# Up projections of a two-block transformer on one Trainium2 core: weights split over PSUM, quarter sums made and stored by GpSimd, modulation weights loaded by SP

## The chip, the cores and the metric

The kernel runs on one core of one Trainium2 chip. The metric is the device time of one execution in microseconds (us). A core has TensorE (matmuls, written to PSUM), VectorE (DVE in the rows), ScalarE (ACT), GpSimd (POOL), and SyncE (SP, which here only issues DMAs). Each engine works through its own instructions in order. PEld is the loading of weights into TensorE.

## The reference

Two transformer blocks on x of 1 x 1024 x 1024, float32. Each block ends with a feed-forward part whose first matmul, the up projection, is what the change is about:

```python
# first block
h = rms_norm(x, ffn_pre_norm[l])
f = jnp.square(jax.nn.relu(h @ w_up[l])) @ w_down[l]        # w_up 1024 x 4096
x = x + rms_norm(f, ffn_post_norm[l])
# second block, with a modulation from c
mod = c @ w_ada[l] + b_ada[l]                               # w_ada 1024 x 6144, six rows of 1024
sh1, sc1, gt1, sh2, sc2, gt2 = jnp.split(mod, N_MOD, axis=-1)
h = modulate(rms_norm_2(x, g_pre_mix[l]), sh1, sc1)
...
h2 = modulate(rms_norm_2(x, g_pre_mlp[l]), sh2, sc2)
ff = jnp.square(jax.nn.relu(h2 @ w_mlp_in[l])) @ w_mlp_out[l]
x = x + gt2[:, None, :] * rms_norm_2(ff, g_post_mlp[l])
```

## The kernel before

**Products in three matmuls.** Every float32 operand is split into a high part (hi, rounded to the matmul's format) and a low part (lo, the rest). One product of two operands is hi x hi + hi x lo + lo x hi, so 3 matmuls per 128 rows of the contraction (mm3, L173). Without a scale, `split` is a ScalarE copy for hi (L178) and a VectorE subtraction for lo (L179).

**Seven products in place of eight.** Both matmuls of the feed-forward part use a 2 x 2 block scheme with seven block products and sums of blocks (Strassen's, in Winograd's form). `ffn_up` walks over 16 slabs of 256 columns of w_up (`slab`, L1061). For each slab it loads 1 MB of weights with SP (L1065), alternately into the buffers `w_raw` and `fraw`; VectorE makes four sums of weight blocks (`fws`, L1073); `halves_of` splits them and the raw blocks into the `w_hi` and `w_lo` tiles, two of each, which is one slab's worth. Then follow the products q6, q2, q7, q5, q4, q3 with 12 matmuls of 128x512 each, into the six PSUM banks of the `mm` ring. VectorE adds them up:

- u2 = x + q6 (L1098, tile `fu2`), f11 = x + q2 (L1103, tile `f00`), u3 = u2 + q7 (L1109, `fu3`), f22 = u3 + q5 (L1113, tile `f11`), f12 = u3 - q4 (L1119, in place in `fu3`), f21 = u2 + q5 + q3 (L1122, L1125, in place in `fu2`).

ScalarE applies relu and the square to f11, f22, f12, f21 (L1050, L1051). f11 and f22 are stored by ScalarE's queue. Then VectorE makes five quarter sums of the squares (L1130, tile `fs`), and SP stores each (L1043) to the scratch tensors fs0, fs4, fs6, fs1, fs5. The down projection (`ffn_down`) reads them back as left operands; there GpSimd makes the sums of weight blocks (L1173).

The products that need only b11 and b21 (p1 and q2) of the first 12 slabs (`LEAD`) are computed ahead, stored to `fx_dr` and loaded back as `fx` and `f00`. So the first 12 slabs run five products in the slab and the last four run seven.

**Buffers.** `TAGS["fp"]` gives the number of buffers of each tile in this stage: `fws`, `fraw`, `fu2`, `fu3`, `f11` have one each, `fx`, `f00`, `fs` two, `ada_acc` two, `ada_raw` one. The PSUM ring `tr` (two banks) holds transposes in other stages and is not used inside a slab.

**Modulation.** mod = c @ w_ada is made by VectorE: `modulation_acc` loads 512 KB of w_ada at a time by GpSimd's DMA queue (L1234, tile `ada_raw`) and adds up the rows weighted by c in `ada_acc` (L1238, L1240). A third runs beside the first up projection (4 column blocks, `side1`), the rest beside the qkv projections of the second block (8 blocks, `block2_conv_qkv`); both are generators that are stepped once per slab or part.

**The order.** A scheduler orders each engine's instructions when the program is built, within the dependences. An instruction that waits holds back all that stands behind it on its engine, DMA issues too.

Of the kernel before, what the change touches and what calls it, by code (L numbers as in the profile page):

```python
# [65 lines left out]
def tile_two_blocks(ctx: ExitStack, tc: tile.TileContext, I, out):  # L66
# [972 lines left out]
    def ffn_up(hq, w_up, fl, fp, first, side):  # L1039
# [20 lines left out]
        def slab(c, lead):  # L1060
# [15 lines left out]

            def halves_of(t, slots, v):
                split(t[0][:, slots], t[1][:, slots], v)

# [3 lines left out]
            if not lead:  # L1083
                halves_of(u[0], slice(2, 4), r4[:, :, 0])
            halves_of(u[0], slice(0, 2), ws[:, 0:2])
            halves_of(u[1], slice(0, 2), ws[:, 2:4])
            halves_of(u[1], 2, a22)
            if lead:
                x, f11 = (fp.tile([P, 512], F32, name=nm) for nm in ("fx", "f00"))
                for i, t in enumerate((x, f11)):  # L1090
                    SP.dma_start(t, fx_dr[:, 512 * (2 * c + i):512 * (2 * c + i) + 512])
                q2 = f11
            else:
                x = p1(fp, op(u[0], 2))
# [32 lines left out]
            for i, x, z, o in ((4, f11, f12, ALU.add), (0, f11, f22, ALU.add), (6, f12, f22, ALU.subtract),  # L1127
                               (1, f21, f22, ALU.add), (5, f21, f11, ALU.subtract)):
                t = fp.tile([P, 512], F32, name="fs")
                DVE.tensor_tensor(out=t, in0=x, in1=z, op=o)  # L1130
                left(c, i, t)

# [95 lines left out]

    def modulation_acc(i, pool, first, prev):

        acc = pool.tile([P, 512], F32, name="ada_acc")
        for q in range(4):
            raw = pool.tile([P, 2, 512], F32, name="ada_raw")
            POOL.dma_start(raw, I["w_ada_2"][0][256 * q:256 * q + 256, 512 * i:512 * i + 512]  # L1234
                           .rearrange("(k p) n -> p k n", p=P))
            for k in range(2):
                if q + k == 0:
                    DVE.tensor_scalar(acc, raw[:, 0, :], col(R_C), None, ALU.mult)  # L1238
                else:
                    DVE.scalar_tensor_tensor(out=acc, in0=raw[:, k, :], scalar=col(R_C + 2 * q + k), in1=acc,  # L1240
                                             op0=ALU.mult, op1=ALU.add)
            if q == 1:
                if i > first:
                    modulation_sum(i - 1, prev, pool)
                yield
        return acc

    def modulation_sum(i, acc, pool):
        row = pool.tile([P, 512], F32, name="f_r")[0:1, :]
        p = mm_tile()  # L1250
        PE.matmul(p[0:1, :], ones[:, 0:1], acc, start=True, stop=True)
        ACT.copy(row, p[0:1, :])
        SP.dma_start(mod_raw[i // 2:i // 2 + 1, (i % 2) * 512:(i % 2) * 512 + 512], row)
# [19 lines left out]
    def modulation(pool, m0, m1):  # L1273

        acc = None
        for i in range(2 * m0, 2 * m1):
            acc = yield from modulation_acc(i, pool, 2 * m0, acc)
            yield
        modulation_sum(2 * m1 - 1, acc, pool)
        modulation_columns(pool, m0, m1)  # L1280
        yield
# [7 lines left out]
    def block2_conv_qkv(h, w_in, pb, first, side):  # L1289
# [6 lines left out]
        def slab(c0, fn):  # L1296
            w = w_cols(w_in, c0, 256)
            for sl in halves:
                part(w, sl, fn)
                next(side, None)  # L1300

# [9 lines left out]
        for pr in range(2):  # L1311
# [5 lines left out]
            for n, sl in enumerate(halves):  # L1317
# [4 lines left out]
                if pr == 0:  # L1322
                    values(n)
                next(side, None)
            for j in range(2):
# [220 lines left out]
    with ExitStack():  # L1546
        with banks(mm=6, tr=2):
# [7 lines left out]
            def side1(fp):  # L1555
                g = modulation(fp, 0, 2)
                return lambda c: next(g, None)

# [9 lines left out]
            with sbuf("dp", 1, tags=TAGS["dp"]) as dp:  # L1568
                with sbuf("yf", 1, side="right") as yp, sbuf("ep", 1, side="right", tags="gpost xt*2 junk yg hmod*2") as ep:
# [6 lines left out]
                        lambda i: w_cols(w_in2, (1024, 512)[i], 256))  # L1576
            with sbuf("pb", 2) as pb, sbuf("pm", 1, tags="ada_acc*2 ada_raw*3 f_r") as pm:
                side = modulation(pm, 2, 6)
# [61 lines left out]
```

## Time and profile before

| | |
|---|---|
| median of 3 runs | 2814.18 us (2810.9 to 2832.78) |
| profiled execution | 2828.66 us, span of its trace 2827.0 us, granted clock 0.975 |
| TensorE busy | 2654.5 us, 94% |
| VectorE busy | 1971.4 us, 70% |
| ScalarE busy | 1309.2 us, 46% |
| GpSimd busy | 564.5 us, 20% |
| first up projection's slabs | about 720 to 1020 us |
| second up projection's slabs | about 2215 to 2500 us |

A busy TensorE is not TensorE at its peak: its matmuls are pipelined and their ends are modelled. Durations of single instructions overlap a little with the next one's. Idle time of an engine is put down to what ended it, the releaser; idle time of an engine that is not the bottleneck costs nothing.

### The profile page before, as it was taken

What the parts mean: (1) busy time and instruction counts of PE and PEld (TensorE: products, weight loads), DVE (VectorE), ACT (ScalarE), POOL (GpSimd) and SP (SyncE); (2) the same over time, 40 slices, a digit from 0 to 9 for tenths busy, and PEclk for the clock granted to TensorE, in tenths of its full rate; (3) what the DMA queues carried; (4) which work ended last, traced back from release to release, by engine and by line L of the source; (5) the groups of instructions that cost most, each with busy time, mean ns of one, the idle gap of its engine ahead of it and who ended that gap; (6) DMA issues with size and microseconds to landing.
All of it is one profiled execution on the core that took longest, in us unless ns stands there. A gap on an engine that the chain in (4) does not pass through costs nothing.

```text
span 2827.0 us, 39450 instructions
## 1 busy us (share of the span) xinstructions
PE 2654.5 (94%) x13801; PEld 2240.7 (79%) x13801; DVE 1971.4 (70%) x3614; ACT 1309.2 (46%) x2360; POOL 564.5 (20%) x568
## 2 busy tenths in 40 slices
PE   8999999999878899999999999998999889999996
PEld 7788889998756687777888788887798767778785
DVE  7668689858777775568764448777567778755666
ACT  5544666546433444345521246564257544443342
POOL 1242353200000022434210013111200000023413
PEclk9999999999989999999999999998999999999998
DMA  4296476356676467777564645443756556487785
GB/s 130 85 295 195 153 214 176 113 168 223 217 229 203 164 243 251 267 257 269 186 219 135 216 135 168 126 117 121 252 180 215 184 192 208 171 301 248 262 281 185
DMA packets 381500, 562.23 MB, mean 199 GB/s; under 512 B 39427, under 2 KB 215658, under 8 KB 381302
## 3 DMA queue, kind: packets, MB, share of 16 engines
q1 hardware_dynamic: 358262, 505.17, 54.3%
q0 software_dynamic: 6912, 25.17, 3.0%
q10 hardware_dynamic: 16128, 29.37, 2.8%
q8 instruction: 109, 1.79, 0.3%
q14 instruction: 89, 0.73, 0.1%
HBM read 408.83 MB, written 150.78 MB: 198 GB/s over the span
## 4 chain that ended last, share of the span: by engine, by line
PE 25%; DMA 17%; DVE 10%; ACT 4%; POOL 4%; issue 3%; SPq 1%; POOLq 0%; DVEq 0%; ACTq 0%
PE mm L173 21%; DMA w_raw<-in_w_down 3%; DVE w_lo L179 3%; DMA w_raw<-in_w_mlp_out 3%; POOL w_raw L1173 3%; DMA fs<-fs 2%; ACT w_hi L178 2%; DMA dwr<-in_w_mlp_out 1%; DMA dwr<-in_w_down 1%; PE po L906 1%; DVE w_lo L209 1%; POOL dwr L1173 1%; PE tr L898 1%; DMA mrg<-m_sg 1%; DMA m_sg<-sig 1%
## 5 line engine op out<-in xcount | busy, mean ns | idle before, releaser
L173 PE MATMUL mm<-w_hi,df 128*128 128x512 f32 x1792 | 559.9, 393 | 9.8 <-ACT y L1200 6.1
L173 PE MATMUL mm<-hq_t,w_hi 128*128 128x512 f32 x1280 | 411.0, 406 | 68.4 <-DVE fu L1098 61.9
L173 PEld LDWEIGHTS mm<-w_hi,df 128*128 128x128 f32 x1792 | 338.6, 189 | 83.9 <-ACT y L1200 7.3
L173 PE MATMUL mm<-w_lo,df 128*128 128x512 f32 x896 | 352.8, 394 | 8.4 <-DVE w_lo L179 8.3
L173 PEld LDWEIGHTS mm<-hq_t,w_hi 128*128 128x128 f32 x1280 | 249.4, 196 | 131.8 <-DVE fu L1098 37.7
L173 PE MATMUL mm<-h_hi,w_hi 128*128 128x512 f32 x736 | 290.9, 395 | 0.0
L173 PE MATMUL mm<-h_lo,w_hi 128*128 128x512 f32 x736 | 289.4, 393 | 0.0
L173 PE MATMUL mm<-h_hi,w_lo 128*128 128x512 f32 x736 | 289.0, 393 | 0.0
L173 PE MATMUL mm<-hq_t,w_lo 128*128 128x512 f32 x640 | 253.5, 402 | 1.6 <-DVE w_lo L179 1.6
L209 DVE TENSOR_TENSOR w_lo<-w_raw,w_hi 128x1024 fp32r<-128x1024 f32 (+1 forms) x138 | 172.5, 1273 | 98.2 <-ACT w_hi L203 97.9
L1173 POOL TENSOR_TENSOR w_raw<-w_raw 128x1024 f32<-128x1024 f32 x40 | 109.0, 2725 | 580.1 <-DMA fs<-fs 392.2
L203 ACT CAST w_hi<-w_raw 128x1024 fp32r<-128x1024 f32 (+1 forms) x138 | 139.1, 1049 | 172.3 <-PE mm L173 68.9
L173 PEld LDWEIGHTS mm<-w_lo,df 128*128 128x128 f32 x896 | 169.7, 189 | 49.0 <-DVE w_lo L179 14.2
L173 PE MATMUL mm<-w_hi,mixT 128*128 128x256 f32 x1024 | 184.9, 282 | 5.2 <-DVE m_sg L1443 2.2
L179 DVE TENSOR_TENSOR df<-dfr,df 128x1024 fp32r<-128x1024 f32 x112 | 147.1, 1324 | 56.5 <-ACT df L178 56.3
L179 DVE TENSOR_TENSOR w_lo<-dwr,w_hi 128x1024 fp32r<-128x1024 f32 x56 | 105.2, 1879 | 114.1 <-ACT w_hi L178 113.7
L1173 POOL TENSOR_TENSOR dwr<-dwr 128x1024 f32<-128x1024 f32 x40 | 99.6, 2491 | 372.4 <-DMA dwr<-in_w_mlp_out 200.5
L173 PEld LDWEIGHTS mm<-h_hi,w_hi 128*128 128x128 f32 x736 | 138.4, 188 | 33.9 <-issue 2.8
L173 PEld LDWEIGHTS mm<-w_hi,mixT 128*128 128x128 f32 x1024 | 157.7, 189 | 7.2 <-ACT w_hi L203 4.7
L173 PEld LDWEIGHTS mm<-h_hi,w_lo 128*128 128x128 f32 x736 | 138.4, 188 | 27.3
L173 PEld LDWEIGHTS mm<-h_lo,w_hi 128*128 128x128 f32 x736 | 138.4, 188 | 26.3 <-issue 0.2
L173 PE MATMUL mm<-hq,w_hi 128*128 128x512 f32 x512 | 159.2, 391 | 0.0
(415 smaller groups left out, 5850.3 us busy)
## 6 DMA issues: line engine op xcount, KB each, us to landing
dfr<-fs SPq DMA_DIRECT2D x112, 512.0 KB
fs<-fs SPq DMA_DIRECT2D x160, 256.0 KB
w_raw<-in_w_in SPq DMA_DIRECT2D x32, 1024.0 KB
ada_raw<-in_w_ada POOLq DMA_DIRECT2D x48, 512.0 KB, 5.1
w_raw<-in_w_down SPq DMA_DIRECT2D x48, 512.0 KB
dwr<-in_w_down SPq DMA_DIRECT2D x48, 512.0 KB
w_raw<-in_w_mlp_out SPq DMA_DIRECT2D x48, 512.0 KB
dwr<-in_w_mlp_out SPq DMA_DIRECT2D x48, 512.0 KB
```

Source lines behind the costliest of these rows:

```text
L173: PE.matmul(ps, l, r, start=first and n == 0, stop=final and n == last)
L178: ACT.copy(hi, src)
L179: DVE.tensor_tensor(out=lo, in0=src, in1=r32(hi), op=ALU.subtract)
L203: ins = ACT.copy(wh[:, step * i:step * i + step], raw[:, step * i:step * i + step])
L209: DVE.tensor_tensor(out=wl[:, c], in0=raw[:, c], in1=r32(wh[:, c]), op=ALU.subtract)
L898: PE.transpose(pt[:, 256 * j + P * i:256 * j + P * i + P], prob[i][:, ks], ident)
L906: PE.matmul(po[:, d:], vb if j else va, t[:, 256 * j:256 * j + 256 - d], start=n == 0 and m == 0, stop=n == len(groups) - 1 and m == 3)
L1173: POOL.tensor_tensor(out=a, in0=a, in1=b, op=ALU.subtract if sub else ALU.add)
```

## The change

Four things change, all in or beside the up projections.

- `halves_of` now works on one block of 128 x 512 at a time. ScalarE copies the block to `w_hi` and then copies `w_hi` again into a bank of the `tr` ring in PSUM; VectorE subtracts with one operand in PSUM. The order of the blocks changes: s4 is split last.
- The five quarter sums are made by GpSimd (its `tensor_tensor`) and stored from GpSimd's DMA queue. The `fs` buffers stay two.
- The modulation weights are loaded by SP. In the first up stage `ada_raw` has two buffers and `ada_acc` one.
- The modulation steps once per 512 KB load in place of once per two; the callers in `block2_conv_qkv` step it twice, and the last slab of the first up projection runs it to its end. The row of a finished block goes through an `fs` buffer in place of one of its own.

```diff
@@ TAGS
-    "fp": "fws fraw fx*2 f00*2 fu2 fu3 f11 fs*2 ada_acc*2 ada_raw f_r",
+    "fp": "fws fraw fx*2 f00*2 fu2 fu3 f11 fs*2 ada_acc ada_raw*2",
@@ slab
-            def halves_of(t, slots, v):
-                split(t[0][:, slots], t[1][:, slots], v)
+            def halves_of(t, n, v):
+
+                ACT.copy(t[0][:, n], v)
+                pt = tr_tile().rearrange("p (k n) -> p k n", k=4)
+                ACT.copy(pt, r32(t[0][:, n]))
+                DVE.tensor_tensor(out=t[1][:, n], in0=v, in1=pt, op=ALU.subtract)
...
             if not lead:
-                halves_of(u[0], slice(2, 4), r4[:, :, 0])
-            halves_of(u[0], slice(0, 2), ws[:, 0:2])
-            halves_of(u[1], slice(0, 2), ws[:, 2:4])
+                halves_of(u[0], 2, a11)
+                halves_of(u[0], 3, a12)
+            halves_of(u[0], 0, s2)
+            halves_of(u[0], 1, s3)
+            halves_of(u[1], 0, s1)
             halves_of(u[1], 2, a22)
+            halves_of(u[1], 1, s4)
...
                 t = fp.tile([P, 512], F32, name="fs")
-                DVE.tensor_tensor(out=t, in0=x, in1=z, op=o)
-                left(c, i, t)
+                POOL.tensor_tensor(out=t, in0=x, in1=z, op=o)
+                left(c, i, t, POOL)
@@ modulation_acc
             raw = pool.tile([P, 2, 512], F32, name="ada_raw")
-            POOL.dma_start(raw, I["w_ada_2"][0][256 * q:256 * q + 256, 512 * i:512 * i + 512]
+            SP.dma_start(raw, I["w_ada_2"][0][256 * q:256 * q + 256, 512 * i:512 * i + 512]
...
-            if q == 1:
-                if i > first:
-                    modulation_sum(i - 1, prev, pool)
-                yield
+            yield
@@ modulation_sum
-        row = pool.tile([P, 512], F32, name="f_r")[0:1, :]
+        row = pool.tile([P, 512], F32, name="fs")[0:1, :]
@@ block2_conv_qkv, twice
-                next(side, None)
+                next(side, None), next(side, None)
```

The scheduler moves instructions as a consequence. Three places show it. Numbers behind a name tell the tiles of one slab from those of another; lines of the changed kernel are up to 12 higher than those of before, and u2 is L1105 there.

VectorE before, first up projection, end of one slab and start of the next: the fs rows are the five quarter sums of a slab, and the L1098 row is u2 of the next.

```order
L1130 TENSOR_TENSOR fs_10522<-f00_10431,f11_10481 128x512 [waits DMAHW3_49,Activation_49]
L1130 TENSOR_TENSOR fs_10519<-f00_10431,fu3_10466 128x512 [waits DMAHW0_49,Activation_49]
L1130 TENSOR_TENSOR fs_10528<-fu2_10447,f11_10481 128x512 [waits DMAHW7_49,DVE_49,Activation_49]
L1130 TENSOR_TENSOR fs_10525<-fu3_10466,f11_10481 128x512 [waits DMAHW0_49,DVE_49]
L179 TENSOR_TENSOR w_lo_10685<-fws_10679,w_hi_10684 128x1024 [waits PE_49,Activation_49]
L1130 TENSOR_TENSOR fs_10531<-fu2_10447,f00_10431 128x512 [waits DMAHW3_49,DVE_49]
L1098 TENSOR_TENSOR fu2_10582<-fx_10565,mm_10569 128x512 [waits DVE_49]
L1109 TENSOR_TENSOR fu3_10601<-fu2_10582,mm_10588 128x512 [waits DVE_49]
```

The sums wait for the DMAs of their buffers in VectorE's own row, and u2 stands behind the last of them.

VectorE in the changed kernel, the same place in another slab, from u2 to the subtraction of f12 (L1126):

```order
L1105 TENSOR_TENSOR fu2_10089<-fx_10072,mm_10076 128x512 [waits Pool_49]
L1082 TENSOR_TENSOR w_lo_10190<-fws_10182,tr_10208 128x512 [waits Activation_49]
L1116 TENSOR_TENSOR fu3_10108<-fu2_10089,mm_10095 128x512 [waits DVE_49]
L1073 TENSOR_TENSOR fws_10327<-fraw_10325 128x512 [waits DMAHW3_49,DVE_49]
L1110 TENSOR_TENSOR f00_10212<-fx_10211,f00_10212 128x512 [waits DMAHW5_49,DMAHW1_49,DMAHW0_49]
L1073 TENSOR_TENSOR fws_10327<-fraw_10325 128x512
L1120 TENSOR_TENSOR f11_10123<-fu3_10108,mm_10110 128x512 [waits DMAHW6_49,DVE_49]
L1129 TENSOR_TENSOR fu2_10089<-fu2_10089,mm_10110 128x512
L1073 TENSOR_TENSOR fws_10327<-fws_10327,fraw_10325 128x512 [waits DVE_49]
L1126 TENSOR_TENSOR fu3_10108<-fu3_10108,mm_10128 128x512 [waits DVE_49]
```

u2 now waits for GpSimd, and here nine operations stand from u2 to f12; in the slab ahead of it five do. Over the 16 slabs the count is 7.5 on average in the first stage and 6.25 in the second.

GpSimd in the changed kernel, one slab of the first up projection and the first sum of the next (before, its row held only the loads of `ada_raw` here):

```order
L1137 TENSOR_TENSOR fs_10025<-f00_9934,f11_9984 128x512 [waits DMASW1_49,Activation_49]
L1043 DMA fs0_99<-fs_10025 128x512 [waits Pool_49]
L1137 TENSOR_TENSOR fs_10022<-f00_9934,fu3_9969 128x512 [waits DMASW7_49,Activation_49]
L1043 DMA fs4_103<-fs_10022 128x512 [waits Pool_49]
L1137 TENSOR_TENSOR fs_10031<-fu2_9950,f11_9984 128x512 [waits DMASW2_49,Activation_49]
L1043 DMA fs1_100<-fs_10031 128x512 [waits Pool_49]
L1137 TENSOR_TENSOR fs_10028<-fu3_9969,f11_9984 128x512 [waits DMASW3_49]
L1043 DMA fs6_105<-fs_10028 128x512 [waits Pool_49]
L1137 TENSOR_TENSOR fs_10034<-fu2_9950,f00_9934 128x512 [waits DMASW5_49]
L1043 DMA fs5_104<-fs_10034 128x512 [waits Pool_49]
L1137 TENSOR_TENSOR fs_10164<-f00_10073,f11_10123 128x512 [waits DMASW6_49,Activation_49]
```

Each sum waits for the store (DMASW) of an earlier one, since the five share two buffers in turn: fs4, fs6 and fs5 of this slab have the one, fs0 and fs1 the other. fs5 is the last reader of `fu2`.

## Rows read from the trace of the kernel before

**Rows 1.** The windows view, by stage; after the stretch: length, then each engine.

```profile
core 0: us, PE busy (x) PEld busy (x) DVE busy (x) ACT busy (x) POOL busy (x), PEclk, DMA share, GB/s
720.00:1020.00 300.00, 254.05 (x1039) 202.11 (x1038) 230.38 (x334) 120.33 (x185) 14.18 (x17) 0.92 0.59 195
...
1350.00:1650.00 300.00, 295.22 (x1471) 244.18 (x1469) 156.35 (x248) 80.94 (x135) 35.33 (x48) 1.00 0.57 189
2215.00:2500.00 285.00, 261.25 (x1103) 211.99 (x1102) 218.12 (x306) 125.56 (x186) 9.96 (x5) 0.97 0.57 198
```

**Rows 2.** Groups of instructions, 720 to 1020 us: busy, mean ns, idle before.

```profile
line engine op names shapes xcount | busy us, mean ns | idle before us <-releasers
L173 PE MATMUL mm<-hq_t,w_hi 128*128 128x512 f32 x608 | 196.9, 409 | 46.0 <-DVE fu L1098 41.4 <-ACT hq_t L356 3.3 <-ACT fx L1057 0.7
...
L179 DVE TENSOR_TENSOR w_lo<-fws,w_hi 128x1024 fp32r<-128x1024 f32 x32 | 39.0, 1219 | 1.3 <-ACT w_hi L178 1.3
...
L1130 DVE TENSOR_TENSOR fs<-fu,f 128x512 f32<-128x512 f32 x44 | 31.6, 730 | 30.9 <-DMA fs<-fs 30.9
...
L1098 DVE TENSOR_TENSOR fu<-fx,mm 128x512 f32<-128x512 f32 x15 | 10.3, 684 | 1.8 <-PE mm L173 1.5
...
L1057 ACT COPY fx<-mm 128x512 f32<-128x512 f32 x4 | 2.3, 583 | 2.9 <-PE mm L173 2.9
```

**Rows 3.** The chain of waits, 1460 to 1600 us: start, us, what.

```profile
1466.92 32.87 PE mm L173 x144
```

**Rows 4.** Timeline, VectorE: first and last of 16 L1098, per stage.

```profile
734.96 0.69 DVE L1098 TENSOR_TENSOR fu<-fx,mm 128x512 f32<-128x512 f32 x1 [1.50 <-PE mm L173]
...
1025.37 0.69 DVE L1098 TENSOR_TENSOR fu<-fx,mm 128x512 f32<-128x512 f32 x1
...
2216.99 0.68 DVE L1098 TENSOR_TENSOR fu<-fx,mm 128x512 f32<-128x512 f32 x1
...
2480.20 0.69 DVE L1098 TENSOR_TENSOR fu<-fx,mm 128x512 f32<-128x512 f32 x1
```

**Rows 5.** Timeline, VectorE, 874 to 882 us: start, us, line, out<-in, idle before.

```profile
874.42 0.68 DVE L1130 TENSOR_TENSOR fs<-f,f 128x512 f32<-128x512 f32 x1
...
877.22 1.42 DVE L1130 TENSOR_TENSOR fs<-fu,f 128x512 f32<-128x512 f32 x2 [1.41 <-DMA fs<-fs]
...
880.78 0.69 DVE L1130 TENSOR_TENSOR fs<-fu,f 128x512 f32<-128x512 f32 x1 [1.01 <-DMA fs<-fs]
881.51 0.69 DVE L1098 TENSOR_TENSOR fu<-fx,mm 128x512 f32<-128x512 f32 x1
```

**Rows 6.** Timeline, ScalarE, same slab.

```profile
886.28 0.62 ACT L1051 ACTIVATE fu<-fu 128x512 f32<-128x512 f32 x1
```

**Rows 7.** What tile fs waits for: us, times.

```profile
  DMA fs<-fs: 71.6, 43
```

**Rows 8.** Line 1234: duration ns min/median/max; landing of its loads; who waited.

```profile
L1234 POOL DMA_DIRECT2D ada_raw<-in_w_ada x48: 722/722/928, 730.8 to 1605.4; - x48
...
  DVE ada_acc L1240: 20.9, 15
...
DMA to landing us min/median/max: 4.0/5.1/7.7
```

**Rows 9.** Timeline from the start: SP's first 512 KB load and its reader.

```profile
0.81 0.39 SPq L254 DMA_DIRECT2D xt<-in_x  x1
...
4.41 1.06 ACT L274 ACTIVATE xj<-xt 128x1024 f32<-128x1024 f32 x1 [2.32 <-DMA xt<-in_x]
```

**Rows 10.** Line 629, GpSimd sums of 128x512: duration ns min/median/max.

```profile
L629 POOL TENSOR_TENSOR cacc<-cacc,cprod x16: 1270/1290/2377, 247.4 to 361.0; 128x512 f32<-128x512 f32 x16
```

**Rows 11.** Tile dwr: duration ns min/median/max of GpSimd sums and VectorE subtractions.

```profile
L179 DVE TENSOR_TENSOR w_lo<-dwr,w_hi x56: 1211/1226/3468, 1027.9 to 2792.8; 128x1024 fp32r<-128x1024 f32 x56
...
L1173 POOL TENSOR_TENSOR dwr<-dwr x40: 2370/2396/3288, 1022.4 to 2788.7; 128x1024 f32<-128x1024 f32 x40
```

**Rows 12.** The page, groups: the same subtraction's mean over the run.

```profile
L179 DVE TENSOR_TENSOR w_lo<-dwr,w_hi 128x1024 fp32r<-128x1024 f32 x56 | 105.2, 1879 | 114.1 <-ACT w_hi L178 113.7
```

More of the change, by code (lines that the diff above doesn't have):

```diff
@@ L1226, in ffn_down, with modulation_acc @@
         return res
-    def modulation_acc(i, pool, first, prev):
+    def modulation_acc(i, pool):
         acc = pool.tile([P, 512], F32, name="ada_acc")
@@ L1276, in modulation @@
         for i in range(2 * m0, 2 * m1):
-            acc = yield from modulation_acc(i, pool, 2 * m0, acc)
-            yield
+            if acc is not None:
+                modulation_sum(i - 1, acc, pool)
+            acc = yield from modulation_acc(i, pool)
         modulation_sum(2 * m1 - 1, acc, pool)
@@ L1323, in block2_conv_qkv @@
                     values(n)
-                next(side, None)
+                next(side, None), next(side, None)
             for j in range(2):
@@ L1556, in side1, with step @@
                 g = modulation(fp, 0, 2)
-                return lambda c: next(g, None)
+                def step(c):
+                    next(g, None)
+                    if c == 15:
+                        for _ in g:
+                            pass
+                return step
             mx1 = ExitStack()
@@ L1576, in tile_two_blocks @@
                         lambda i: w_cols(w_in2, (1024, 512)[i], 256))
-            with sbuf("pb", 2) as pb, sbuf("pm", 1, tags="ada_acc*2 ada_raw*3 f_r") as pm:
+            with sbuf("pb", 2) as pb, sbuf("pm", 1, tags="ada_acc*2 ada_raw*3 fs") as pm:
                 side = modulation(pm, 2, 6)
```

## The prediction, made before the changed kernel was run

> **What bounds the kernel now.** I read the windows view first, for the two stretches that the change touches: the up projection of the first block (720 to 1020 us) and of the second (2215 to 2500 us) [rows 1]. TensorE is busy 254 of 300 us and 261 of 285 us there, and its granted clock is 0.92 and 0.97 of full speed, a mean over its two levels (1.2 and 2.4 GHz). Elsewhere at full clock one 128x512 matmul takes 32.87/144 = 0.228 us [rows 3], so the 1039 and 1103 matmuls of these windows need 237 and 252 us. 63 and 33 us are lost, 96 us together: that is all that any relief of the other engines can win here.
>
> Then the groups of the first window, for what TensorE waits for. 41.4 of the 46.0 us of idle time before the hq_t matmuls end with VectorE's L1098 [rows 2], the first sum of a slab (u2 below). u2 starts 16 times in a stage, from 734.96 to 1025.37 us and from 2216.99 to 2480.20 us [rows 4]: 15 steps of 19.4 us and 15 of 17.5 us. One slab of the first twelve has five products of 12 matmuls, 60 x 0.228 = 13.7 us; one of the last four has seven, 19.2 us. So the early slabs are paced by something else than TensorE.
>
> It is not VectorE's throughput alone: 230 of 300 us are busy [rows 1], about 14 us of a 19.4 us step. Part of the rest is the wait for a free fs buffer, 71.6 us in 43 waits over both stages [rows 7], 30.9 of them before one group in the first window [rows 2]. The timeline of one slab shows how that runs [rows 5]: a sum at 874.42, the next use of its buffer at 877.22, once its store has landed, another wait before 880.78, and only then, behind it in VectorE's row, u2 of the next slab at 881.51.
>
> **The change part by part.**
>
> Quarter sums. Five leave VectorE per slab: 5 x 0.69 us [rows 2], and the waits before them. On GpSimd a 128x512 sum takes 1.29 us [rows 10] and a DMA issue 0.72 us [rows 8], so 5 x 2.01 = 10 us of engine time per slab: it fits a step of 17 us. But fu2 has one buffer and its last reader is the fifth sum, so in the changed order u2 waits for GpSimd, and the sums alternate on two fs buffers. That makes a ring, which I cost as follows:
> - From u2 to the squared f12: 881.51 [rows 5] to 886.28 + 0.62 = 886.90 [rows 6], 5.4 us, where five VectorE operations lie from u2 to the subtraction of f12.
> - Then fs4 needs f12, fs6 needs fs4's buffer back, fs5 needs fs6's buffer back, and u2 needs fs5: three sums, 3.9 us, and two returns of a buffer, 2K. K is the time from a sum's end to its store landed.
> - So a step is 9.3 us + 2K. Operations that the new order puts between u2 and f12 add 0.6 us each. It has 7.5 places on average in the first stage and 6.25 in the second, instead of five: 1.5 and 0.75 us. Half the slabs have a copy and a cast of ScalarE among the squares too, 2 x 0.58 us [rows 2]: 0.5 us on average.
>
> K for a store of 256 KB by GpSimd stands in no row. From below: SP's store took from 874.42 + 0.68 to 877.22, 2.1 us [rows 5]. From above: GpSimd's loads of 512 KB land 5.1 us after issue in the median [rows 8]. Between them: GpSimd's quickest 512 KB load took 4.0 us [rows 8], SP's first one 4.41 - 0.81 = 3.6 us [rows 9], so GpSimd's way costs some 0.4 us more: 2.5 us unhindered. Under this load the median is 5.1/4.0 of the quickest: 3.2 us, and 0.1 us for the hand-over. I take K = 3.3 us, nearer the store than the load, since bytes and direction are the store's.
> The Trainium skill (DMA: Bandwidth & Descriptors, section Anatomy of one DMA) gives a GpSimd DMA 2.0 us + bytes/436e3, an estimate of 2.6 us for 256 KB and 3.2 us for 512 KB; this trace does not agree, its quickest 512 KB load is 4.0 us. By the page's 2.6 us the sum below would be 42 us lower.
>
> With K = 3.3 the steps are 9.3 + 6.6 + 1.5 + 0.5 = 17.9 us and 17.15 us. Against 19.4 and 17.5 us over 15 steps each: -22 us and -6 us.
>
> Subtractions from PSUM. VectorE took 1.22 us for 1024 columns [rows 2]; now it takes two of 512 at the 0.68 us of an operation with one PSUM operand (L1098) [rows 2]. With five slots in an early slab that is 3.4 us for 3.1 us: no relief. ScalarE adds five copies; the nearest row is 0.58 us (PSUM read, 128x512) [rows 2], so 2.9 us, and some 0.4 us for the split casts. No row has ScalarE writing to PSUM; bounds 0 and twice that, 1.16 us each, and I take the row. ScalarE is busy 120 of 300 us [rows 1], 8 us of a step, so it is then at 11 to 14 us and still off the path: cost 0. VectorE falls to about 11 us a slab, plus 1.5 us of modulation in the first stage.
>
> Modulation weights. 48 issues leave GpSimd for SP. Two raw buffers in the first stage could save the waits of VectorE, 20.9 us in both modulations [rows 8]; if the ring paces, they are not on the path: 0, and at best -13 us. SP gains 16 loads in the first stage and loses 80 stores in each, which waited there for VectorE. A load of ada_raw at SP's head that waits for VectorE holds w_up behind it; the ring's slack (17 against 13.7 us) covers one such wait of 3 us. In the second modulation (1350 to 1650 us) TensorE is busy 295 of 300 us and VectorE 156 [rows 1]: nothing is late, 0; without that cover the 32 loads would cost 0.4 us of SP each.
>
> The end of the up stage. Ten sums of the last two slabs now stand in GpSimd's row among the first eight weight sums of the down projection (2.4 us each [rows 11]). A weight sum can be kept by one store's return and one sum, 3.3 + 1.3 us; I count 5 us per stage, ends 0 and 10: +10 us.
>
> Sum: -22 - 6 + 10 = -18 us. On the profiled execution's own 2828.66 us (span 2827.0 us) that is 2811 us. The median of the runs is 2814.18 us, 14.5 us lower, so there it is **2796 us**, -0.6%. About 1%, 28 us, is what a measurement of this kernel can tell from no change.
>
> **The rivals.**
>
> *The stores return quickly.* K near 2.5 us: thirty steps lose 2 x 0.8 us each, 48 us more, 2748 us. For it: stores no longer share SP's queue with loads of 1 MB, and SP's own took 2.1 us. Against it: the loaded median of GpSimd's loads. Its end is TensorE's pace, all 96 us: 2718 us. Here the step would be VectorE's 11 us or TensorE's 13.7 us, and GpSimd would only have moved work off.
>
> *The stores return slowly: slower than before.* One mechanism, K: each us is 60 us of the kernel. It turns the sign at K = 3.6 us and passes 1% slower at K = 4.1 us. With 4.5 us, still below the median of the 512 KB loads, the time is 2868 us. For it: GpSimd issues only after its own sum, so that the issue's 0.72 us lies inside K, where SP's overlapped VectorE's next work. Against: half the bytes.
>
> *Sums and VectorE hold each other.* VectorE's w_lo over dwr takes 1226 ns in the median and 3468 ns at most [rows 11], 1879 ns on average [rows 12], while GpSimd's sums run beside it and stretch from 2396 to 3288 ns [rows 11]: 0.65 us per operation. In an early slab the operations with two SBUF operands are four fws sums and one f00 sum; some two of five lie between u2 and f12, 2 x 0.65 us x 30 = 39 us, 2835 us. Against it: the subtractions and the other sums read PSUM.
> The Trainium skill (SBUF — State Buffer, section Who interferes with whom) says that a VectorE instruction with two SBUF inputs contends with a GpSimd instruction that reads SBUF; the stretched rows agree.
>
> *The change does not do what it says*: if VectorE were the bound, the PSUM subtractions would not relieve it (3.4 for 3.1 us); only the sums do.
>
> **How the numbers follow.** Ring at K between 3.1 and 4.1 us, 2786 to 2842 us, likeliest 2796: chance 0.38. Quick stores: 0.35. Slow stores: 0.17. Contention on top of the forecast: 0.10, of which 0.06 stay within 1%. So faster 0.35, within 1% 0.44, slower 0.21. The range leaves out a tenth on either side: K below 2.45 us, 2745 us, and K above 4.2 us, 2850 us.
>
> **What would show it.** After the change: u2 preceded by idle time that ends with GpSimd's fs; GpSimd's sums preceded by idle time that ends with their own stores; u2's steps near 17.9 and 17.2 us; VectorE some 100 us less busy (160 sums at 0.69 us); TensorE still idle behind u2. Steps of 14 to 15 us would prove the ring quick. The forecast is wrong if u2 does not wait for GpSimd, if K is outside 3.1 to 4.1 us, or if ScalarE's copies come last before the matmuls.

## The result, and the profile after

The changed kernel took 2897.01 us in the median of 4 runs (2887.93 to 2906.47), the kernel before 2817.55 us in 4 runs beside it (2810.9 to 2832.78): a ratio of 1.0275, 95% interval 1.0218 to 1.0332. It is slower by 2.8%, above the upper end of the range (2850 us), where 2796 us had been forecast. The profiled execution has a span of 2890.4 us, against 2827.0 us before: 63.4 us more. Medians and ratios below are of fast executions; one slow one of e9 (5313 us) and one of e13 (3260 us) are left out.

The windows view, the two up stages, to be held against [rows 1]:

```profile
core 0: us, PE busy (x) PEld busy (x) DVE busy (x) ACT busy (x) POOL busy (x), PEclk, DMA share, GB/s
720.00:1020.00 300.00, 241.19 (x977) 191.43 (x976) 187.63 (x283) 159.93 (x292) 131.38 (x137) 0.90 0.54 185
...
2215.00:2500.00 285.00, 228.29 (x936) 182.94 (x935) 159.45 (x241) 153.58 (x283) 119.57 (x128) 0.91 0.49 169
```

VectorE is relieved as meant (187.6 for 230.4 us), and yet TensorE issues 977 matmuls where 1039 stood, and 936 for 1103. In these windows no engine is full: this is a loop of waits, not a lack of throughput. Over the whole run VectorE is busy 1898.6 us, 73 us less than before, where some 100 us less had been forecast.

Groups of the first stage (columns as in [rows 2]):

```profile
L173 PE MATMUL mm<-hq_t,w_hi 128*128 128x512 f32 x590 | 193.6, 412 | 58.3 <-DVE fu L1105 49.0 <-ACT hq_t L356 5.5 <-ACT fx L1057 1.4
...
L1137 POOL TENSOR_TENSOR fs<-fu,f 128x512 f32<-128x512 f32 x41 | 54.7, 1334 | 49.7 <-DMA fs<-fs 47.7 <-ACT f L1051 1.6
L1081 ACT COPY tr<-w_hi 128x512 f32<-128x512 f32 x85 | 48.0, 583 | 5.0 <-DVE w_lo L1082 4.9
L1082 DVE TENSOR_TENSOR w_lo<-fws,tr 128x512 fp32r<-128x512 f32 x61 | 40.9, 685 | 61.4 <-ACT tr L1081 61.0
...
L1073 DVE TENSOR_TENSOR fws<-w_raw 128x512 f32<-128x512 f32 x14 | 12.9, 962 | 0.1
...
L1105 DVE TENSOR_TENSOR fu<-fx,mm 128x512 f32<-128x512 f32 x14 | 9.6, 684 | 26.4 <-POOL fs L1137 24.8 <-PE mm L173 1.5
```

TensorE still waits for u2 (49.0 us). u2, which waited for almost nothing before, now waits for GpSimd's sums (24.8 us), and these for their stores (47.7 us): the three links of the ring stand one under the other. The page's row of these matmuls over the whole run, shown with e14 below, says the same with 103.2 us that u2 ended. The tile view of `fs` shows the stores' issues and the waits for their return:

```profile
L1043 POOL DMA_DIRECT2D fs<-fs x160: 539/557/767, 745.3 to 2585.5; - x160
...
  DMA fs<-fs: 123.9, 54
...
  DVE fu L1105: 63.8, 17
```

The page's row of the same stores has the median from issue to landing, 2.6 us:

```profile
fs<-fs POOLq DMA_DIRECT2D x160, 256.0 KB, 2.6
```

Against [rows 7], the waits for free `fs` buffers rose from 71.6 to 123.9 us; they moved from VectorE to GpSimd and grew. First and last u2 of each stage on VectorE's timeline, to be held against [rows 4]:

```profile
735.06 0.69 DVE L1105 TENSOR_TENSOR fu<-fx,mm 128x512 f32<-128x512 f32 x1 [1.50 <-PE mm L173]
...
1057.10 0.68 DVE L1105 TENSOR_TENSOR fu<-fx,mm 128x512 f32<-128x512 f32 x1
...
2237.76 0.68 DVE L1105 TENSOR_TENSOR fu<-fx,mm 128x512 f32<-128x512 f32 x1
...
2552.72 0.68 DVE L1105 TENSOR_TENSOR fu<-fx,mm 128x512 f32<-128x512 f32 x1
```

Fifteen steps of 21.47 us and fifteen of 21.00 us, where 17.9 and 17.15 had been forecast and 19.36 and 17.55 stood before: 15 x 2.11 + 15 x 3.45 = 83.4 us lost between first and last u2. By the last u2 of the first stage and the first u2 of the second, 11.0 us are regained behind the first stage; behind the second it is 9.1 us, and 0.1 us is lost ahead of the first u2: 83.4 - 20.0 = 63.4 us, the whole difference of the two spans.

Two GpSimd stretches show how a buffer comes back. The quick way, from fs6 to fs5 on the same buffer (timeline: start, us, line, idle before):

```profile
2396.80 1.30 POOL L1137 TENSOR_TENSOR fs<-fu,f 128x512 f32<-128x512 f32 x1
2398.40 0.56 POOL L1043 DMA_DIRECT2D fs<-fs  x1 [0.30 <-POOL fs L1137]
2400.75 1.29 POOL L1137 TENSOR_TENSOR fs<-fu,f 128x512 f32<-128x512 f32 x1 [1.79 <-DMA fs<-fs]
```

fs6 ends at 2398.10; 0.30 us later the store is issued, and 2.35 us after that fs5 starts: 2.65 us from a sum's end to the next start on its buffer, called a return below. The slow way, in an earlier slab of the same stage:

```profile
2263.49 0.56 POOL L1043 DMA_DIRECT2D fs<-fs  x1 [0.30 <-POOL fs L1137]
2264.07 1.30 POOL L1137 TENSOR_TENSOR fs<-f,fu 128x512 f32<-128x512 f32 x1
2265.67 0.56 POOL L1043 DMA_DIRECT2D fs<-fs  x1 [0.30 <-POOL fs L1137]
2270.59 1.28 POOL L1137 TENSOR_TENSOR fs<-fu,f 128x512 f32<-128x512 f32 x1 [4.36 <-DMA fs<-fs]
2272.39 1.29 POOL L1137 TENSOR_TENSOR fs<-fu,f 128x512 f32<-128x512 f32 x1 [0.52 <-DMA fs<-fs]
2273.63 1.09 POOL L1043 DMA_DIRECT2D fs<-fs  x2
2281.04 1.26 POOL L1137 TENSOR_TENSOR fs<-fu,f 128x512 f32<-128x512 f32 x1 [6.32 <-DMA fs<-fs]
```

fs0 starts at 2261.91, fs4 is the sum at 2264.07, then follow fs1, fs6 and fs5. fs4 ends at 2265.37 and fs6 can start only at 2272.39. Two things stand between: fs1, which is ahead of it in the row, waits 4.36 us for the other buffer, whose store had been issued at 2263.49 and landed 7.0 us later; and fs4's own store lands 6.7 us after its issue, so that fs6 waits another 0.52 us behind fs1. fs1 ends at 2271.87, but its store is issued at 2273.63, since the next sum stands ahead of the issue; fs6's store is issued behind it and takes 6.8 us to land, and fs5 starts 7.4 us after fs6's end.

Over the 15 + 15 steps the two returns fs4 to fs6 and fs6 to fs5, 60 in all, have a median of 3.33 us and a mean of 4.36 us: 32 take 2.6 to 3.4 us, 28 take 3.5 to 9.9 us. By the landing of each store in the trace, the mean divides into 0.56 us from the sum's end to the store's issue (0.30 us where nothing stands between), 3.35 us from issue to landing, and 0.45 us from landing to the next sum. The last part is GpSimd's own row: in 13 of the 30 cases fs4 to fs6 takes 3.05 to 3.1 us, because fs1 and two issues stand between, and the store had landed 0.4 to 0.5 us earlier.

### The profile page after: what moved, and what is told of

Read it like the earlier page. It is cut to its first block, busy times and chain, and to the rows that moved or that the text cites. A ratio compares the mean times of both kernels' runs of the same rounds, so it can differ in the third digit from the quotient of the medians.

```text
span 2890.4 us, 39700 instructions
## 1 busy us (share of the span) xinstructions
PE 2659.9 (92%) x13801; PEld 2242.6 (78%) x13801; DVE 1898.6 (66%) x3526; ACT 1404.9 (49%) x2608; POOL 833.3 (29%) x840
## 4 chain that ended last, share of the span: by engine, by line
PE 22%; DMA 13%; DVE 8%; ACT 5%; POOL 4%; issue 4%; SPq 0%; POOLq 0%; ACTq 0%; DVEq 0%
PE mm L173 19%; DMA dwr<-in_w_mlp_out 3%; DMA fs<-fs 3%; DVE w_lo L179 2%; POOL fs L1137 2%; POOL dwr L1180 1%; PE po L906 1%; DVE w_lo L209 1%; PE tr L898 1%; ACT w_hi L178 1%; DMA w_raw<-in_w_mlp_out 1%; DMA mixR<-mrg 1%; POOL w_raw L1180 1%; DMA m_sg<-sig 1%; ACT w_hi L203 1%
## 5 line engine op out<-in xcount | busy, mean ns | idle before, releaser
L173 PE MATMUL mm<-w_hi,df 128*128 128x512 f32 x1792 | 560.6, 393 | 20.8 <-ACT w_hi L178 13.5
L173 PE MATMUL mm<-hq_t,w_hi 128*128 128x512 f32 x1280 | 415.9, 408 | 114.1 <-DVE fu L1105 103.2
L179 DVE TENSOR_TENSOR df<-dfr,df 128x1024 fp32r<-128x1024 f32 x112 | 160.3, 1445 | 87.1 <-ACT df L178 86.9
L173 PEld LDWEIGHTS mm<-w_lo,df 128*128 128x128 f32 x896 | 169.7, 189 | 49.9 <-DVE w_lo L179 15.4
L1137 POOL TENSOR_TENSOR fs<-f,f 128x512 f32<-128x512 f32 x32 | 43.9, 1372 | 469.1 <-ACT f L1051 459.7
L1082 DVE TENSOR_TENSOR w_lo<-fws,tr 128x512 fp32r<-128x512 f32 x128 | 85.6, 685 | 140.5 <-ACT tr L1081 139.6
L179 DVE TENSOR_TENSOR w_lo<-dwr,w_hi 128x1024 fp32r<-128x1024 f32 x56 | 104.6, 1869 | 101.4 <-ACT w_hi L178 101.0
L178 ACT CAST df<-dfr 128x1024 fp32r<-128x1024 f32 x112 | 115.6, 1050 | 108.8 <-PE mm L173 75.6
L1137 POOL TENSOR_TENSOR fs<-fu,f 128x512 f32<-128x512 f32 x96 | 129.6, 1352 | 114.0 <-DMA fs<-fs 110.3
```

The lines of the kernel that those rows point to most:

```text
L173: PE.matmul(ps, l, r, start=first and n == 0, stop=final and n == last)
L178: ACT.copy(hi, src)
L179: DVE.tensor_tensor(out=lo, in0=src, in1=r32(hi), op=ALU.subtract)
L1082: DVE.tensor_tensor(out=t[1][:, n], in0=v, in1=pt, op=ALU.subtract)
L1137: POOL.tensor_tensor(out=t, in0=x, in1=z, op=o)
```

## The experiments

All but one are edits of the changed kernel. The table gives each one's median, its ratio to the kernel before on the same chip with the 95% interval, and the mean step from u2 to u2 in the two stages (15 steps each). The kernel before stands at 2822 to 2824 us in these comparisons, and at 2818 us in that of the changed kernel itself. Two `fu2` buffers together with two of `ada_raw`, or five of `fs` with two of `ada_raw`, don't fit the memory of the stage, so the runs with more buffers have one `ada_raw`.

| run | sums, stores | buffers fu2 / fs / ada_raw | us | ratio (interval) | steps |
|---|---|---|---|---|---|
| before | VectorE, SP | 1 / 2 / 1 | 2823 | 1 | 19.4, 17.5 |
| after | GpSimd, GpSimd | 1 / 2 / 2 | 2897 | 1.0275 (1.0218 to 1.0332) | 21.5, 21.0 |
| e1 | VectorE, SP | 1 / 2 / 2 | 2814 | 0.9962 (0.9947 to 0.9977) | 19.0, 18.1 |
| e6 (on before) | GpSimd, GpSimd | 1 / 2 / 1 | 2890 | 1.0229 (1.0208 to 1.0250) | 22.2, 20.7 |
| e2 | GpSimd, SP | 1 / 2 / 2 | 2841 | 1.0053 (1.0035 to 1.0071) | 19.5, 18.9 |
| e3 | GpSimd, GpSimd | 1 / 4 / 1 | 2835 | 1.0047 (1.0026 to 1.0067) | 19.7, 17.5 |
| e8 | GpSimd, no return | 1 / 2 / 2 | 2828 | 1.0017 (1.0005 to 1.0029) | 17.7, 17.0 |
| e9 | last two slabs VectorE, SP | 1 / 2 / 2 | 2886 | 1.0229 (1.0203 to 1.0255) | 20.8, 20.6 |
| e14 | GpSimd, GpSimd | 2 / 2 / 1 | 2797 | 0.9923 (0.9892 to 0.9954) | 17.1, 16.1 |
| e10 | GpSimd, GpSimd | 2 / 3 / 1 | 2772 | 0.9827 (0.9797 to 0.9857) | 16.2, 15.2 |
| e11 | VectorE, SP | 1 / 4 / 1 | 2759 | 0.9771 (0.9753 to 0.9789) | 16.1, 15.1 |
| e12 (split as before) | VectorE, SP | 1 / 4 / 1 | 2761 | 0.9790 (0.9767 to 0.9813) | 16.7, 15.4 |
| e13 | VectorE, SP | 2 / 3 / 1 | 2747 | 0.9747 (0.9721 to 0.9773) | 16.2, 15.0 |
| e15 | VectorE, SP; idle sums on GpSimd | 1 / 3 / 1 | 2790 | 0.9889 (0.9868 to 0.9911) | 17.2, 16.3 |

**Which part costs: e1 and e6.** e1 is the change without GpSimd's sums:

```diff
-                POOL.tensor_tensor(out=t, in0=x, in1=z, op=o)
-                left(c, i, t, POOL)
+                DVE.tensor_tensor(out=t, in0=x, in1=z, op=o)
+                left(c, i, t)
```

> The change without its second part: VectorE makes the five quarter sums and SP stores them, as before; the split over PSUM and the modulation loads by SP stay. Theory R (the ring of GpSimd's sums, two fs buffers and one fu2 buffer paces a slab at 21 us): the whole loss leaves with the sums, so 2800 to 2835 us, steps of u2 near 17.5 to 19 us as before. Theory S (ScalarE's five more copies per slab, or the PSUM ring of two banks, pace it): most of the loss stays, 2860 to 2900 us. Theory M (the modulation loads hold SP's weight loads up): about half of it stays, in the first stage alone.

e6 is the opposite: the kernel before with only these two lines changed.

> The kernel before with one edit: GpSimd makes and stores the quarter sums. Theory R: the loss is there in full, 2870 to 2910 us. Theory S: no loss, 2800 to 2830 us. Contention of two-operand subtractions (which here still read SBUF twice) with GpSimd's sums would add to R, up to 0.65 us on five operations per slab, 2900 to 2960 us.

The sums alone bring 1.0229, all else together 0.9962. So the loss is the sums' own; the subtractions from PSUM, ScalarE's copies and the modulation loads on SP cost nothing together: without the sums they gain 0.4%, and on top of the sums they move the ratio from 1.0229 to 1.0275, where the intervals overlap. e6's steps divide much as those of the changed kernel do: from u2 to fs4 8.6 and 8.1 us in the two stages, three sums 4.2 and 4.3, two returns 8.6 and 7.5, from fs5 to u2 0.8 and 0.8.

**Which link: e2 and e3.** e2 keeps the sums on GpSimd and lets SP store them.

```diff
-                left(c, i, t, POOL)
+                left(c, i, t)
```

> GpSimd makes the sums, but SP stores them. Theory R: the ring has the same links; a store by SP returns its buffer 2.1 us after the sum at best, against 2.9 us for GpSimd's, so up to 2 x 0.8 us less per step where SP is free, and as much more where SP stands behind a wait of its own: 2840 to 2900 us, VectorE still idle before u2 until GpSimd's sum. Theory P (VectorE's operations with two SBUF operands hold up GpSimd's issue of its DMAs, 2.9 us in one long step of the second stage): that gap goes, 32 slabs x about 1.5 us, 2840 to 2855 us.

e3 gives four `fs` buffers; for room `ada_raw` goes back to one.

```diff
-... fs*2 ada_acc ada_raw*2
+... fs*4 ada_acc ada_raw
```

> The changed kernel with four fs buffers in place of two; to make room ada_raw has one buffer in the first up stage. Theory R: no sum waits for a store, so the step is 6.4 us from u2 to the squared f12, then four sums and three issues on GpSimd, 7.8 us, and the hand-over, some 14.6 us in a direct slab and 17 us in a long one: the steps fall from 21 to 16 us and the time to 2740 to 2790 us, below that of the kernel before. Theory S: no change, 2880 to 2900 us. If only half the waits for stores were in the ring: 2830 us.

Both take back most of the loss: a return, and what holds back its issue, is on the path. In e2 the two returns together take 6.4 and 6.8 us a step in the two stages, where 8.6 and 8.9 us stood, and the steps fell by about as much (2.0 and 2.1 us). Its 2841 us lies in the ranges of both theories R and P and doesn't tell them apart; the quickest of GpSimd's returns is 2.6 us, not 2.9.

e3 did not fall to the time expected of it, and its sums were not free of waits for stores either. With four buffers fs6 follows fs4 at once, but the fifth sum takes fs4's buffer again: GpSimd's sums still wait 23.6 us in 16 for stores (119.7 us in 49 in the changed kernel), and in 22 of the 30 steps fs5 starts within 0.2 us of the landing of fs4's store. That store's issue, which stands behind the next sums in GpSimd's row, comes 2.4 and 2.0 us after fs4's end in the mean of the two stages. So fs4 to fs5 takes 5.8 and 5.4 us, where two returns and fs6 took about 10 us. u2 waits 12.4 us in 6 for GpSimd's sums, where it was 63.8 us in 17; the subtractions of the next slab's weights, which stand ahead of it, wait 116.0 us in 60 for ScalarE's copies (165.6 us in 58 in the changed kernel). The rest of the step grew: from u2 to fs4 9.2 and 7.9 us, from fs5 to u2 2.0 and 1.5 us.

**No return at all: e8.** The five stores read the squared f11, so that a sum's buffer is free at once. The scratch then holds no sums.

```diff
-                left(c, i, t, POOL)
+                left(c, i, f11, POOL)
```

> The changed kernel, but each of GpSimd's five stores reads the squared f11 (tile f00) in place of its quarter sum, so a sum's buffer is free at once: the same sums on GpSimd, the same 256 KB stores from the same queue, no wait for a return. The scratch holds no sums then, so the result is not the reference's. Theory return (the ring with two returns of 4.1 to 4.5 us per step, measured in the changed kernel): both returns go from the step, 21.5 and 21.0 us become 7.8 to 8.3 us to fs4, then five sums and issues at GpSimd's own pace, 13 to 15 us; with 30 steps about 190 us less, limited by TensorE's pace: 2725 to 2760 us. Theory GpSimd itself (its sums, issues and the contention with VectorE set the step, the return is only beside them): 2840 to 2900 us.

The theory that the returns are all of it fell: 2828 us, not 2725 to 2760 us. It had asked for more than there was: TensorE's matmuls wait 104.6 us for u2 in the changed kernel and still 37.0 us in e8; that is 68 us less, and the span is 69 us shorter. (The steps themselves fell by 117 us in all; 48 us of that came back outside them, nearly all behind the last u2 of the two stages, which no run takes apart.) VectorE's and GpSimd's timelines of one slab show one thing that is new in e8 (two fences, same kernel):

```profile
2376.70 6.13 DVE L1073 TENSOR_TENSOR fws<-fraw,fws 128x512 f32<-128x512 f32 x1
2382.75 1.27 DVE L1082 TENSOR_TENSOR w_lo<-fws,tr 128x512 fp32r<-128x512 f32 x2
```

```profile
2374.55 2.68 POOL L1043 DMA_DIRECT2D fs<-f  x5 [7.18 <-ACT f L1051]
2377.25 1.30 POOL L1137 TENSOR_TENSOR fs<-f,f 128x512 f32<-128x512 f32 x1
2378.50 1.30 POOL L1137 TENSOR_TENSOR fs<-f,fu 128x512 f32<-128x512 f32 x1
2379.76 4.20 POOL L1137 TENSOR_TENSOR fs<-fu,f 128x512 f32<-128x512 f32 x3
```

One VectorE sum of two SBUF tiles, else 0.68 us, lasts 6.13 us, through more than four of GpSimd's five sums, which without waits follow each other closely. Four of e8's 128 weight sums last 4.9 to 6.1 us. The subtraction with one operand in PSUM keeps its pace beside the same sums (0.64 us each). The Trainium skill (SBUF — State Buffer, section Who interferes with whom) says that a VectorE instruction with two SBUF inputs contends with a GpSimd instruction that reads SBUF, and that one with at most one SBUF input, outside its two-port modes, does not; the rows agree with both. Two things keep e8 from pricing the return cleanly: all five issues can now stand ahead of the sums (2.68 us here), and the hold lies ahead of u2.

**The hold by itself: e15.** Sums on VectorE, and GpSimd makes five idle sums a slab whose results nobody reads, so that what they cost is the hold of VectorE, or of f11's buffer, which they read.

```diff
+            for _ in range(5):
+                d = fp.tile([P, 512], F32, name="fd")
+                POOL.tensor_tensor(out=d, in0=f11, in1=f11, op=ALU.add)
```

> Sums on VectorE with SP stores, three fs buffers, and in each slab GpSimd makes five further sums of the squared f11 with itself into a tile that nobody reads: the load of the change's sums on GpSimd without any wait for it. Theory contention (a VectorE sum of two SBUF tiles stands still while GpSimd's sums run, seen as single sums of up to 6.13 us in place of 0.68): such long sums appear in each slab and the time is 20 to 60 us above the kernel with four buffers, 2780 to 2820 us. Rival (contention lies in slack): 2755 to 2770 us.

2790 us: 30.7 us above e11, which has one `fs` buffer more. In the first stage's groups of VectorE:

```profile
L1073 DVE TENSOR_TENSOR fws<-fraw 128x512 f32<-128x512 f32 x16 | 15.1, 980 | 0.1
L1073 DVE TENSOR_TENSOR fws<-w_raw 128x512 f32<-128x512 f32 x14 | 14.9, 1104 | 0.0
```

These sums take 0.68 us in the kernel before. The longest took 1.53 us: holds of 6 us did not come up, though the five idle sums follow each other without a gap. VectorE's own quarter sums, two SBUF tiles each, are held here as well, and e15 has a buffer less, so its 30 us is likely more than the hold costs the change, which no run shows. The changed kernel's own trace bounds the direct part: its 128 weight sums of both stages last 13.9 us longer in all than at 0.684 us each (three of the six groups of the first stage have means of 962, 965 and 796 ns, the others 0.69 us). And a hold is not always paid: in e10 below the weight sums are held 50.6 us in all, more than the 46.3 us of e8, and it is the fastest kernel here with its sums on GpSimd.

**Which buffer closes the ring: e14 and e10.** e14 gives `fu2` a second buffer and leaves the returns as they are.

```diff
-... fu2 fu3 f11 fs*2 ada_acc ada_raw*2
+... fu2*2 fu3 f11 fs*2 ada_acc ada_raw
```

> The changed kernel with two fu2 buffers, fs left at two, one ada_raw buffer: the returns stay as they are, only u2 no longer closes the ring. Theory ring over fu2: a store's return costs nothing as long as 2.5 sums and returns per buffer fit the step, 2.5 x (1.3 + 4.3) = 14 us: steps near 16 us, 2780 to 2810 us. Rival (the returns hold GpSimd's row, and with it fu3 and f11, whose single buffers close the ring in its place): steps of 18 us and more, 2830 us or above.

e10 has three `fs` buffers besides.

> The changed kernel with two fu2 buffers, three fs buffers and one ada_raw buffer: u2 no longer waits for the fifth sum of the slab before. Theory fu2 (the ring closes over fu2 alone): the steps fall to between TensorE's 13.7 us and 16 us, 2740 to 2780 us. Rival 1 (the ring then closes over fu3, which fs6 reads last, and is 2 to 3 us shorter than over fu2): steps of 16 to 17 us, 2780 to 2820 us. Rival 2 (GpSimd's sums keep the pace whatever buffer closes the ring): near the 2835 us of four fs buffers.

One more buffer for `fu2` is worth 100 us (1.0275 to 0.9923), with the same stores from the same queue and one `ada_raw` less. The returns were no quicker: the stores land 3.3 us after issue in the median (2.6 us in the changed kernel), and the waits for free `fs` buffers even grew:

```profile
  DMA fs<-fs: 147.8, 72
```

But u2 waits only 4.2 us in 4 for GpSimd's sums, where it was 63.8 us in 17: a return costs what it does here because `fu2` has one buffer. The pages' rows of the matmuls that use `hq_t`, for after, e14 and e10:

```profile
L173 PE MATMUL mm<-hq_t,w_hi 128*128 128x512 f32 x1280 | 415.9, 408 | 114.1 <-DVE fu L1105 103.2
```

```profile
L173 PE MATMUL mm<-hq_t,w_hi 128*128 128x512 f32 x1280 | 399.9, 397 | 32.9 <-DVE fu L1116 18.2
```

```profile
L173 PE MATMUL mm<-hq_t,w_hi 128*128 128x512 f32 x1280 | 393.7, 394 | 9.9 <-ACT hq_t L356 4.5
```

In e14 the largest wait is for u3 (L1116), which has taken u2's place; in e10 it is gone. No run gives a second `fu2` alone to the kernel with its sums on VectorE, so what it would bring there is not shown.

**The transition: e9.** VectorE makes the sums of the last two slabs of a stage, and SP stores them.

```diff
+                q = (DVE, SP) if c >= NC - 2 else (POOL, POOL)
+                q[0].tensor_tensor(out=t, in0=x, in1=z, op=o)
+                left(c, i, t, q[1])
```

> The changed kernel, but the sums of the last two slabs of each stage are made by VectorE and stored by SP, so that no sum stands among the weight sums of the down projection. Theory transition (the last step of a stage, 30.2 and 29.3 us against 17.0 and 17.9 before, comes from GpSimd's row, where the weight sums and these sums hold each other): last steps of 18 to 22 us, about 20 us less in all, 2872 to 2882 us. Rival (the last step is long because the ring is long there for another reason, such as the seven products of the last slabs or the down projection's loads): 2892 to 2900 us.

The last steps fell from 30.2 and 29.4 us to 19.9 and 20.0 us as the theory said, but the time only to 2886 us, and the intervals of the two ratios overlap. The long last step had cost little: the work behind it caught up, by the 20 us regained above.

**Sums on VectorE with enough buffers: e11, e12, e13.** e11 is e1 with `fs*4` and one `ada_raw`.

> The changed kernel with the sums back on VectorE, stored by SP, and four fs buffers in place of two (one ada_raw buffer). With two buffers VectorE waited 91 us in 53 waits for the stores' returns. Theory return: the waits go, the steps fall from 19.0 and 18.1 us to 14.5 to 16 us, 2730 to 2775 us, faster than before and than the change. Rival (VectorE's own work and the chain of squares keep the step, the waits lay in slack): 2800 to 2815 us.

e12 is e11 with the weights split as before.

> The kernel that measured 2759 us (sums on VectorE, SP stores, four fs buffers, one ada_raw buffer) with the weights split as before: one ScalarE copy and one subtraction over 1024 columns, both operands in SBUF. The PSUM split is the only difference. By the prediction's step (3.4 for 3.1 us of VectorE, ScalarE off the path: no relief, no cost) 2750 to 2765 us. Rival (the extra ScalarE copies, behind which the subtractions and u2 stand in their rows, hold u2: the shorter chain is quicker): 2735 to 2750 us. Rival (the finer pieces let products start earlier): 2770 us and more.

e13 is e1 with `fu2*2`, `fs*3` and one `ada_raw`.

> Sums on VectorE with SP stores, two fu2 buffers, three fs buffers, one ada_raw buffer. Theory return (on VectorE the waits for stores were the whole loss, fu2 is free in time there): three buffers leave some waits, 2755 to 2775 us, no better than 2759 us. Rival (u2 is held by the fifth sum even on VectorE): steps of 14 us, 2735 to 2750 us.

e11 takes 2.3% off the kernel before, and 1.9% off e1: what held that kernel was in good part the return of two `fs` buffers in VectorE's own row, and buffers cure it. The tile view of `fs`, first in e1, then in e11, counts the waits for returns:

```profile
  DMA fs<-fs: 91.4, 53
```

```profile
  DMA fs<-fs: 33.1, 20
```

e12 against e11: the same within the intervals, so the PSUM split is worth nothing either way, as its term in the sum said. e13 has the lowest median, 2746.76 us, faster than both kernels; that is the rival's range, though its steps of 14 us did not come, and its interval overlaps that of e11, so the second `fu2` buffer is not shown to help with the sums on VectorE. Its windows, and its row of the `hq_t` matmuls:

```profile
720.00:1020.00 300.00, 284.51 (x1201) 225.89 (x1200) 253.88 (x391) 186.22 (x327) 19.55 (x8) 0.98 0.71 243
2215.00:2500.00 285.00, 278.26 (x1209) 226.95 (x1208) 218.99 (x304) 174.35 (x287) 28.91 (x12) 0.99 0.68 231
```

```profile
L173 PE MATMUL mm<-hq_t,w_hi 128*128 128x512 f32 x1280 | 391.7, 394 | 9.8 <-ACT hq_t L356 5.6
```

TensorE is busy 284.5 of 300 us where it was 254 [rows 1]. e13 against e10, which differ only in the engine of the sums and the queue of their stores: by the ratios 0.8%, some 23 us, in favour of VectorE, although it is then 254 of 300 us busy.

## Why the prediction was wrong, point by point

- **What bounds the kernel**: right. The early slabs were not paced by throughput, and the bound of 96 us on all relief holds: e13 wins some 71 us of it by its ratio. (VectorE's share of a 19.4 us step, put at about 14 us, is 14.9 us by [rows 1]; the sum does not rest on it.)
- **The ring over fu2**: right in its mechanism, link by link, and e14 shows it. The sign is decided by its length, and there the sum failed, in three terms. Over the 30 steps 28 us were to be won, and 83 us were lost, 111 us apart:
  - *K*, the return of a buffer, was the step that failed most: 4.36 us in the mean where 3.3 us had been put, +2.0 and +2.3 us a step, 64 of the 111 us. What it left out is mostly GpSimd's row, not the transfer. The 3.2 us for the transfer under load met the mean from issue to landing, 3.35 us, by luck, since they were scaled from loads of twice the size, and the median here is 2.30 us. The hand-over, put at 0.1 us, takes 0.56 us: 0.30 us at least, and more where the next sum stands ahead of the issue. And after the landing the next sum comes 0.45 us later in the mean, since other sums and issues stand ahead of it; for this the sum had nothing. As the prediction defined K, from a sum's end to the store landed, it is 3.91 us, inside the 3.1 to 4.1 us of its own sign: the sum needed the time until the buffer's next sum starts. That the median of these, 3.33 us, is near 3.3 us says nothing for the working. (The issue itself takes 0.56 us, not 0.72.)
  - *From u2 to fs4*: 7.4 and 6.65 us forecast (5.4 with the two additions), 8.28 and 7.84 us measured, +0.9 and +1.2 us, 31 of the 111 us. The step that begins with u2 at 2363.45 shows a long case, 9.3 us to fs4 at 2372.76. In VectorE's row f12 is the ninth operation after u2 and ends at 2369.53; then ScalarE's row has a cast of the next weights ahead of f12's relu, and f21's relu and a copy between f12's relu and square:

```profile
2369.84 0.60 ACT L1079 CAST w_hi<-fws 128x512 fp32r<-128x512 f32 x1
2370.35 1.15 ACT L1050 ACTIVATE fu<-fu 128x512 f32<-128x512 f32 x2
2371.41 0.57 ACT L1081 COPY tr<-w_hi 128x512 f32<-128x512 f32 x1
2371.92 1.14 ACT L1051 ACTIVATE fu<-fu 128x512 f32<-128x512 f32 x2
```

  - *From fs5 to u2*: taken as nothing, 0.60 and 0.32 us measured, 14 of the 111 us. The three sums were near (3.98 us for 3.9).
  - Together +3.6 and +3.9 us, and steps of 21.47 and 21.00 us.
- **u2 has a second master.** The prediction let u2 wait for the ring alone. It waits for GpSimd 17 times of 32; in most of the others it stands behind a subtraction of the next slab's weights, which waits for ScalarE, which waits for TensorE to be done with `w_hi`. ScalarE and VectorE of after, one such step:

```profile
2399.04 0.62 ACT L1079 CAST w_hi<-fws 128x512 fp32r<-128x512 f32 x1 [4.11 <-PE mm L173]
```

```profile
2401.22 0.69 DVE L1082 TENSOR_TENSOR w_lo<-fws,tr 128x512 fp32r<-128x512 f32 x1 [5.49 <-ACT tr L1081]
2401.82 0.68 DVE L1082 TENSOR_TENSOR w_lo<-fraw,tr 128x512 fp32r<-128x512 f32 x1
2402.42 0.68 DVE L1105 TENSOR_TENSOR fu<-fx,mm 128x512 f32<-128x512 f32 x1
```

  fs5 had started at 2400.75 and ended at 2402.04, so there the two loops close within 0.4 us of each other: a shorter ring alone would have won little in such a step. That fits e3 and e8, where the returns were fewer or gone and the time stayed at 2835 and 2828 us. How much of it is this second loop, and how much the hold by GpSimd's sums, is not shown.
- **Subtractions from PSUM, ScalarE copies, modulation loads**: costed at nothing, and e1 and e12 show nothing. ScalarE's write to PSUM, for which no row stood before, takes 583 ns, and the subtraction 685 ns: the rows chosen were right.
- **The transition**: +10 us forecast. The last steps hold 24.6 us (13.2 + 11.4) more than before, the 20.0 us regained leave about 5 us, and e9 moves the time by 11 us, within the uncertainty. The term is not shown to be off by much.
- **The rivals.** *The stores return slowly* is what happened: a mean of 4.36 us at 60 us a piece gives 2860 us by its rule, the other terms the rest. It got 0.17, too little: the bounds of K were the store's 2.1 us and the loads' 5.1 us, and the forecast sat below their middle, 3.6 us, with nothing measured that held it there. The rule of 60 us for each us of K does not hold all the way down: e8 has no return, and the time only fell to 2828 us. By the Trainium skill (DMA: Bandwidth & Descriptors, section Anatomy of one DMA) a GpSimd DMA of 256 KB takes 2.6 us, an estimate from its fit; the stores' median landing of 2.6 us agrees with it, and the mean in this ring, 3.35 us, does not. *Sums and VectorE hold each other* is real, but 39 us was too much for this change: its weight sums are lengthened by 13.9 us in all. e15 (30 us) and e10 against e13 (23 us) hold other things besides. Its argument against, that the subtractions read PSUM, is right for these, but one held weight sum holds the whole row. *The stores return quickly* fell.

## What to carry to other kernels

When work is moved to a slower engine, ask first which buffer's last reader it becomes: here `fu2` with one buffer turned five sums off the path into a ring, and a second buffer was worth 100 us. In a ring of waits a transfer's return counts from the end of the writer to the start of the buffer's next writer, in the mean: its slow tail, the instructions ahead of its issue and those ahead of the next writer are all in it. Where an engine waits for returns of its own stores, try more buffers before another engine: from two to four, with one `ada_raw` less, took 1.9% here (e1 to e11).

## What the runs showed of the hardware that was not expected

- A VectorE sum of two SBUF tiles can be held for the length of several GpSimd sums: 6.13 us for 0.68 us in e8, up to 4.43 us in e3, up to 1.8 us in the changed kernel, where the waits for the stores leave gaps between GpSimd's sums. Gaps alone do not decide it: e15's five sums leave none, and the longest hold of a weight sum there is 1.53 us.
- GpSimd issues a store 0.30 us after the sum that it waits for, also though both are its own, and takes 0.56 us for the issue.
- In 1 of 160 cases the issue came much later with nothing to wait for in the trace: the one at 2382.31 us ends an idle time of 2.88 us, put down to "issue". VectorE's four weight sums of two SBUF tiles end just before, at 2382.09 us, but they are not the cause: it is the 114th DMA that GpSimd issues, and the 114th is late by 1.63 to 2.89 us in e3, e8, e9, e10 and e14 as well, while in e6, where GpSimd also loads w_ada, one is late by 2.22 us (its 176th) with VectorE idle. What is, stays open.
- What makes a landing take 2.3 us or 8.0 us for the same 256 KB was not settled. The medians differ between kernels too: 2.6 us in the changed kernel and 3.3 us in e14 from GpSimd's queue, 5.4 us in e13 from SP's.
